# Hybrid decoder block with a PEER expert layer: row gathers serve 224 tokens instead of 192, and 288 instead of 320 go through all experts

## The chip, the cores and the metric

The kernel runs on one core of a Trainium2 chip. The metric is the device time of one launch in microseconds (us), lower is better. Five engines work side by side and meet through semaphores: TensorE (PE; its weight loads are listed as PEld), VectorE (DVE), ScalarE (ACT), GpSimd (POOL) and SyncE (SP, which issues nearly all plain DMAs). Each engine executes its own queue strictly in order. Sixteen DMA engines move data between HBM and the on-chip memory.

## What is computed

One decoder block for 512 tokens of width 2048, in float32. The first part (convolution and stick-breaking attention, gated and merged) isn't touched by the change. The second part is a PEER layer: every token picks 128 of 16384 experts (8 heads, 16 each), and adds what these experts give.

```python
def peer_ffn(x, wq, subkeys, u_table, v_table):
    q = jnp.einsum("btd,dq->btq", x, wq).reshape(b, t, 8, 2, 128)
    scores = jnp.einsum("bthsc,snc->bthsn", q, subkeys)
    top_s, top_i = lax.top_k(scores, 16)
    ...                                   # 16 best sums of both halves per head
    gate = jax.nn.softmax(sel_s, axis=-1)
    u = u_table[ib]                       # rows of the chosen experts, 128 per token
    hidden = jnp.einsum("td,thkd->thk", xb, u)
    act = jax.nn.gelu(hidden, approximate=False) * gb
    v = v_table[ib]
    return jnp.einsum("thk,thkd->td", act, v)

def reference(...):
    ...                                   # x: residual stream after the mixers
    xn = rmsnorm(x, norm_ffn)
    x = x + peer_ffn(xn, peer_wq, peer_subkeys, peer_u, peer_v)
    return rmsnorm(x, norm_final)
```

## The kernel before

Tokens are served by the PEER layer in two ways. The last 320 tokens (`ND`) go through **all** 16384 experts on TensorE, with a gate plane that is zero where a token didn't choose an expert. The first 192 tokens (`G0`) are served by **row gathers**: an indirect DMA brings, for 128 partitions at a time, one row of 2048 values of the table u or v per partition (1 MB, `fetch`, L685), and VectorE takes it in: for u a product with the token's vector, summed (L696), for v a multiply-add onto a running sum (L703).

The gathers come in two runs. The first serves tokens 0 to 127, one token per partition, 128 slots each: 128 gathers of u and then 128 of v. The second serves 64 tokens (`NG2`) with the slots of each token on two groups of partitions: 64 gathers of u, then 64 of v. At the end of a run `finish` adds the partition groups of the running sum (L757 copies one group's part by DMA, L758 adds it), takes the root mean square of the result with two ScalarE squares that write a PSUM tile of the ring `z` (L193), scales (L725) and stores. The ring `z` has two buffers that are handed out in program order, and the products with v need them too.

A gather needs one of four buffers `row` (`ROWS`); in the v part of a run the running sum holds one of them. The generator `gather` is advanced by `pump(rate)`: each step asks for one gather and takes in the one asked for a step earlier. A unit is 48 matmuls: either one expert tile of the up product (`up`, 16 blocks of the contraction times three products of high and low halves), or a pair of output blocks of the down product (`products`). The dense part has 128 up units and 128 down units: first the 64 up units of the chunks 0 to 7 (their result goes to memory without gates, L800), then the 64 down units of these chunks (`regain` fetches and gates the activations), and then eight chunks with 8 up and 8 down units each. Until the routing and the gate planes are done (unit 60), `pump` gets a rate of 1.0 gather per unit; after that the rate is chosen so that what is left is spread evenly over what is left of the dense part (`even`), less by a tenth up to unit 128. At the start of the last chunk's down product (`"last"`) what is left of the gathers is taken in.

Weights come as halves of 128 x 1024 (512 KB, L148) into seven buffers in the dense part (four `wraw`, three `spare`). ScalarE writes the rounded half `whi` (L133), VectorE the rest `wlo` (L134). Both have three buffers (`WHL`), so TensorE has at most three halves ahead, and each half feeds 24 matmuls. Nothing reaches TensorE in the dense part without a `wlo` from VectorE.

The order of each engine's queue isn't written by hand: a scheduler with a timeline of its own sets it when the program is built. The taking in of gathers is kept in program order among itself (`PIN`).

Of the kernel before, what the change touches and what calls it, by code (L numbers as in the profile page):

```python
# [8 lines left out]
F32 = mybir.dt.float32  # L9
# [21 lines left out]
NE = P // CHUNK  # L31
NG2 = 64
G0 = P + NG2
# [47 lines left out]
def block_kernel(ctx, tc, a, out, dbg=None):  # L81
# [77 lines left out]
    def behind(ins):  # L159
        """Queue ins on its engine behind the latest weight product."""  # L160
        tc.add_manual_dep(ins.ins, pe_last[0].ins.name, mybir.DependencyInfo(mybir.DependencyClass.NoSync, mybir.DependencyReason.DATA), reason="behind")
# [40 lines left out]
    def turn(x2, k, pin):  # L202
        """Two 128-column blocks of the pair of row tiles, transposed: [128, 2, 256]."""
        tp = accum()
        for kk in range(2):
            for tt in range(2):
                o = kk * NH + tt * P
                t = nc.tensor.transpose(tp[:, o:o + P], x2[tt][:, (k + kk) * P:(k + kk) * P + P], ident)
                if pin:
                    behind(t)  # L210
        return tp.rearrange("p (k t) -> p k t", k=2)

    def load_x(h):
        """Transposed tokens of one half times the norm's gains, split; 1 / rms of each token to inv."""
        t0 = h * NH
# [45 lines left out]
    def mixer(h, st, x):  # L261
        """Attention, convolution and their gated merge for one half of the tokens; the merge goes to
        md, and the last of it straight to the tiles of the output projection."""
        xhi, xlo, inv, first = x
# [156 lines left out]
    def suffix(pool, z, sp, seg, nj, W):  # L421
        """z minus the sums of sp over the keys from each key to the end."""
        last = nj - 1
# [21 lines left out]
    def outproj(pool, h, m, box):  # L445
        """Output projection and residual of 256 tokens."""
        t0 = h * NH
# [37 lines left out]
    def chain(pool, h, box, nhi, nlo, c0):  # L485
        """Normalized, transposed and split tokens of one half from column c0; tokens 0.. to xn2d."""
        x2 = box["x2"]
# [34 lines left out]
    def queries(pool, h, st, nhi, nlo, c0):  # L522
        """Product-key scores of 256 tokens, queued for the top 16 of each group."""
        for half in range(2):
            zt = [ztile() for _ in range(2)]
            for cg in range(8):
                ct = half * 8 + cg
                acc = accum()[:, :NH]
                yield from mmk(acc, wtile(a["wq"][ct]), lambda k: nhi[:, k, c0:c0 + NH], lambda k: nlo[:, k, c0:c0 + NH])
                pq = pool.tile([P, NH], F32, name="pq", bufs=2)  # L530
                mark(nc.scalar.copy(pq, acc))
                for tt in range(2):
                    nc.tensor.matmul(zt[tt][:, cg * P:cg * P + P], pq[:, tt * P:tt * P + P], sk[:, ct % 2], start=True, stop=True)
                yield
            both = None if h else row()
            for tt in range(2):
                sc = st["scp"].tile([P, 1024], F32, name="sc", bufs=4) if h else both[:, tt * 1024:tt * 1024 + 1024]
                nc.scalar.copy(sc, zt[tt])
                for cg in range(8):
                    st["topk"][2 * h + tt].append((sc[:, cg * P:cg * P + P], half * 8 + cg))  # L540
# [8 lines left out]
    def route(pool, tile_no, st):  # L549
        """Product-key routing of one 128-token tile: expert halves and gate of each slot."""  # L550
        ls = pool.tile([P, 2, 8, 2, 16], F32, name="ls", bufs=1)
# [10 lines left out]
        nc.vector.tensor_copy(tif, ti)  # L562
        # Of the 16 x 16 sums of two sorted lists only those with (a + 1) * (b + 1) <= 16 can be among
        # the first 16; rows a of widths 16, 8, 4, 1 hold them all, in the order of the full list.
        cand = spare()[:, 0:512].rearrange("p (h c) -> p h c", h=8)
# [14 lines left out]
        eg = pool.tile([P, 3, 8, 16], F32, name="eg", bufs=2)  # L580
        # Position in the compact list -> row a and column b.
        ic = pool.tile([P, 2, 8, 16], U32, name="ic", bufs=1)
# [51 lines left out]
    def gates(pool, eg, p0, b0, nb):  # L634
        """Dense gate planes of 16-token blocks b0.. from tokens on partitions p0.. of a routing tile."""
        for _ in range(GLAG):
# [39 lines left out]
    def gather_tile(pool, np_, nslot, idx, gate, load_x, load_acc, finish):  # L676
        """Row gathers for np_ partitions of (token, slot group), nslot slots each."""
        gx = late[1].tile([P, D], F32, name="gx", bufs=1)[0:np_]
# [49 lines left out]
    def gather(routes):  # L728
        idx = routes[0][0]
        yield from gather_tile(  # L730
            late[1], P, P, idx, st["gate"],
            lambda t: nc.sync.dma_start(t, xn2d[0:P]),
            lambda t: nc.sync.dma_start(t, x2d[0:P]),
            lambda t: finish_rows(t, slice(0, P), final_gain()))
        if not NG2:
            return
        S = P // (P // NG2)
        idx, eg = routes[1]
        idx2 = late[1].tile([P, S], I32, name="idx2")
        gate2 = late[1].tile([P, S], F32, name="gate2")  # L740
        for r in range(P // NG2):
            ps_, ss = slice(r * NG2, r * NG2 + NG2), slice(r * S, r * S + S)
            nc.sync.dma_start(idx2[ps_], idx[0:NG2, ss])
            nc.sync.dma_start(gate2[ps_], eg[0:NG2, 2, ss])

        def load_x(t):
            for r in range(P // NG2):
                nc.sync.dma_start(t[r * NG2:r * NG2 + NG2], xn2d[P:G0])

        def load_acc(t):  # L750
            nc.vector.memset(t, 0.0)
            nc.sync.dma_start(t[0:NG2], x2d[P:G0])

        def finish(t):
            for r in range(1, P // NG2):
                o = row()
                nc.sync.dma_start(o[0:NG2], t[r * NG2:r * NG2 + NG2])  # L757
                nc.vector.tensor_tensor(t[0:NG2], t[0:NG2], o[0:NG2], OP.add)  # L758
            finish_rows(t, slice(P, G0), final_gain())

        yield from gather_tile(late[1], P // NG2 * NG2, S, idx2, gate2, load_x, load_acc, finish)

    def dense(pool, st):
# [18 lines left out]
        def up(ch):  # L782
            """Expert activations of one chunk of expert tiles; without gates in the first chunks."""
            acts = []
# [22 lines left out]
        def regain(ch):  # L807
            """The activations of an early chunk with their gates, in steps that may be spread."""
            gt = gate_planes(ch)
# [93 lines left out]
    pumped = [0]  # L903
    rounds = 2 * P + (2 * (P // (P // NG2)) if NG2 else 0)

# [182 lines left out]
```

## Time and profile before

| | |
|---|---|
| time, three runs | 3630.88, 3636.36 and 3641.12 us, median 3636.36 |
| profiled execution, span from first to last instruction | 3629.1 us |
| TensorE, VectorE, ScalarE, GpSimd busy | 97%, 78%, 45%, 18% |
| DMA traffic | 1056.10 MB, of it 402.68 MB by gathers |

The profile lists no time of its own for the profiled execution beside the span; the span lies 1.8 us under the fastest of the three runs and 7.3 us under their median. Matmuls are pipelined, so a matmul's listed duration is longer than its share of time; what a matmul costs in a row of many is read from counts per stretch. The dense part begins at about 1724 us.

### The profile page before, as it was taken

The page shows a single profiled execution, that of the slowest core. Times are in us where ns is not written, and L with a number is a line of the kernel's source. Part 1 is how long each engine was busy: PE and PEld are TensorE (multiplying, and loading weights), DVE is VectorE, ACT ScalarE, POOL GpSimd, SP SyncE. Part 2 cuts the span into 40 slices and gives each one's busy share as a digit, 9 for nine tenths or more (in the row PEclk, how much of TensorE's full clock was granted, in tenths as well). Part 3 has the DMA queues.
Part 4 walks back from the last instruction along what each step waited for, and adds up shares of the span by engine and source line. Part 5 has one row for each costly group of instructions (what it writes and reads, how often), then busy time and mean ns, then how long its engine had stood idle before and what let it go on. Part 6 is the DMA issues. An engine that isn't in the chain of part 4 may idle for free.

```text
span 3629.1 us, 63343 instructions
## 1 busy us (share of the span) xinstructions
PE 3535.7 (97%) x25347; PEld 3420.6 (94%) x25347; DVE 2833.4 (78%) x4022; ACT 1621.6 (45%) x2277; POOL 644.8 (18%) x520
## 2 busy tenths in 40 slices
PE   9999999999999999889999999999999999999998
PEld 8999999798888999779999999999999999999997
DVE  6555557558988888788999886888887888888885
ACT  5444445445545543554337773333333333333334
POOL 0000000000234222012121111221122322322220
PEclk9999999999999999999999999999999999999998
DMA  5556666663788899899889889899988988889884
GB/s 194 170 176 219 214 216 216 198 193 127 267 306 332 335 344 356 313 331 344 295 324 334 309 317 364 326 358 337 341 328 327 358 328 336 325 338 349 326 319 150
DMA packets 297815, 1056.10 MB, mean 291 GB/s; under 512 B 36464, under 2 KB 109296, under 8 KB 243568
## 3 DMA queue, kind: packets, MB, share of 16 engines
q1 hardware_dynamic: 242224, 649.38, 51.3%
q0 software_dynamic: 55296, 402.68, 28.9%
q8 instruction: 199, 3.26, 0.3%
q14 instruction: 96, 0.79, 0.1%
HBM read 999.98 MB, written 51.38 MB: 290 GB/s over the span
## 4 chain that ended last, share of the span: by engine, by line
PE 73%; DVE 3%; DMA 2%; issue 2%; ACT 1%; POOL 0%; SPq 0%; DVEq 0%; ACTq 0%; POOLq 0%
PE pj L166 13%; PE pj L164 13%; PE pj L165 13%; PE z L164 9%; PE z L165 9%; PE z L166 9%; PE pj L668 2%; DVE wlo L134 1%; PE z L434 1%; PE tr L416 1%; DVE row L696 1%; DMA wraw<-in_w_mix 1%; DMA row<-in_u,idx 1%; PE z L397 0%; DMA gt<-gd 0%
## 5 line engine op out<-in xcount | busy, mean ns | idle before, releaser
L133 ACT ACTIVATE whi<-wraw 128x1024 fp32r<-128x1024 f32 x827 | 874.2, 1059 | 1229.3 <-PE pj L165 726.4
L134 DVE TENSOR_TENSOR wlo<-wraw,whi 128x1024 fp32r<-128x1024 f32 x827 | 1009.2, 1224 | 415.3 <-ACT whi L133 409.5
L166 PE MATMUL pj<-xhi,wlo 128*128 128x256 f32 x2560 | 719.7, 282 | 11.3 <-DVE wlo L134 11.1
L164 PE MATMUL pj<-xhi,whi 128*128 128x256 f32 x2560 | 721.6, 282 | 6.7 <-ACT whi L133 4.7
L165 PE MATMUL pj<-xlo,whi 128*128 128x256 f32 x2560 | 720.5, 282 | 0.0
L164 PE MATMUL pj<-dxhi,whi 128*128 128x320 f32 (+1 forms) x2304 | 710.0, 308 | 2.8 <-ACT whi L133 2.6
L166 PE MATMUL pj<-dxhi,wlo 128*128 128x320 f32 (+1 forms) x2304 | 704.1, 307 | 4.5 <-DVE wlo L134 4.5
L165 PE MATMUL pj<-dxlo,whi 128*128 128x320 f32 (+1 forms) x2304 | 705.8, 307 | 0.0
L164 PE MATMUL z<-ahi,whi 128*128 128x320 f32 x2048 | 631.0, 309 | 4.0 <-ACT z L193 2.9
L165 PE MATMUL z<-alo,whi 128*128 128x320 f32 x2048 | 631.5, 309 | 2.4 <-DVE alo L134 2.4
L166 PE MATMUL z<-ahi,wlo 128*128 128x320 f32 x2048 | 629.6, 309 | 1.8 <-DVE wlo L134 1.8
L166 PEld LDWEIGHTS pj<-xhi,wlo 128*128 128x128 f32 x2560 | 480.0, 188 | 21.5 <-DVE wlo L134 16.1
L164 PEld LDWEIGHTS pj<-xhi,whi 128*128 128x128 f32 x2560 | 481.7, 188 | 12.6 <-ACT whi L133 6.1
L165 PEld LDWEIGHTS pj<-xlo,whi 128*128 128x128 f32 x2560 | 481.4, 188 | 6.7 <-issue 5.3
L685 POOL DMA_INDIRECT row<-in_v,idx x192 | 286.7, 1493 | 1063.8 <-DVE row L703 448.9
L703 DVE SCALAR_TENSOR_TENSOR row<-row,gact 128x2048 f32<-128x2048 f32 x192 | 450.5, 2346 | 19.3 <-DMA row<-in_v,idx 19.3
L696 DVE SCALAR_TENSOR_TENSOR row<-row,gx 128x2048 f32<-128x2048 f32 x192 | 438.4, 2287 | 26.0 <-DMA row<-in_u,idx 25.0
L685 POOL DMA_INDIRECT row<-in_u,idx x192 | 290.8, 1515 | 857.8 <-DVE row L696 213.0
L166 PEld LDWEIGHTS pj<-dxhi,wlo 128*128 128x128 f32 x2304 | 433.3, 188 | 5.6 <-DVE wlo L134 5.6
L164 PEld LDWEIGHTS pj<-dxhi,whi 128*128 128x128 f32 x2304 | 434.5, 189 | 3.2 <-ACT whi L133 2.9
L165 PEld LDWEIGHTS pj<-dxlo,whi 128*128 128x128 f32 x2304 | 434.2, 188 | 0.0
L133 ACT ACTIVATE whi<-spare 128x1024 fp32r<-128x1024 f32 x197 | 208.8, 1060 | 414.8 <-PE z L165 263.8
(232 smaller groups left out, 5019.3 us busy)
## 6 DMA issues: line engine op xcount, KB each, us to landing
wraw<-in_w_in SPq DMA_DIRECT2D x320, 512.0 KB
wraw<-in_uT SPq DMA_DIRECT2D x187, 512.0 KB
wraw<-in_vT SPq DMA_DIRECT2D x128, 512.0 KB
spare<-in_vT SPq DMA_DIRECT2D x128, 512.0 KB
spare<-in_uT SPq DMA_DIRECT2D x69, 512.0 KB
wraw<-in_w_mix SPq DMA_DIRECT2D x64, 512.0 KB
wraw<-in_w_out SPq DMA_DIRECT2D x64, 512.0 KB
wraw<-in_wq SPq DMA_DIRECT2D x64, 512.0 KB
```

The costliest lines, as they stand in the source:

```text
L133: nc.scalar.activation(hi, src, AF.Copy)
L134: nc.vector.tensor_tensor(lo, src, hi.bitcast(F32), OP.subtract)
L164: nc.tensor.matmul(acc, shi, mhi, start=first, stop=False)
L165: nc.tensor.matmul(acc, shi, mlo, start=False, stop=False)
L166: pe_last[0] = nc.tensor.matmul(acc, slo, mhi, start=False, stop=last)
L416: nc.tensor.matmul(yps[hs, q0:], kv[j // 2][1][:, j % 2, hs], e[:, seg(j)], start=j == 0, stop=j == last, skip_group_check=True)
L434: nc.tensor.matmul(z[:, c], stat.bitcast(F32), src[:, c], start=False, stop=True, skip_group_check=True)
L668: behind(nc.tensor.matmul(gp[:, t * P:t * P + P], oh[:, t, 0], oh[:, t, 1], start=True, stop=True))
L685: ins = nc.gpsimd.indirect_dma_start(out=g, out_offset=None, in_=tab, in_offset=bass.IndirectOffsetOnAxis(ap=idx[0:np_, s:s + 1], axis=0))
L696: pin(nc.vector.scalar_tensor_tensor(g, g, 1.0, gx, OP.mult, OP.mult, accum_out=hid[:, s:s + 1]))
L703: pin(nc.vector.scalar_tensor_tensor(acc[0:np_], g, act[:, s:s + 1], acc[0:np_], OP.mult, OP.add))
```

## The change

A table `SEGS` takes the place of the two hand-written runs: three runs of (128 tokens, 1 partition group), (64 tokens, 2 groups) and (32 tokens, 4 groups). The third serves tokens 192 to 223 with 32 gathers of u and 32 of v, and its end has three copies and three additions of partition groups. There are 448 gathers instead of 384. `ND` falls from 320 to 288, so all matmuls of the up and the down product have 288 columns instead of 320, and the tiles of activations, gates and sums shrink alike. The gate planes have 18 blocks of 16 tokens instead of 20. The rate of `pump` after unit 60 follows from the count of gathers left: it was 1.00 rising to 1.04 per unit up to unit 128 and 1.17 after it, and is 1.31 rising to 1.37 and 1.53.

```diff
+SEGS = ((0, 0, 128), (1, 0, 64), (1, 64, 32))
-NG2 = 64
+NG2 = 96
 G0 = P + NG2
 ND = T - G0
...
     def gather(routes):
-        idx = routes[0][0]
-        yield from gather_tile(
-            late[1], P, P, idx, st["gate"],
...
-        yield from gather_tile(late[1], P // NG2 * NG2, S, idx2, gate2, load_x, load_acc, finish)
+        for tile_no, p0, n in SEGS:
+            R = P // n
+            rows = slice(tile_no * P + p0, tile_no * P + p0 + n)
+            idx, eg = routes[tile_no]
+            gate = st["gate"]
+            if R > 1:
...
+                for r in range(R):
+                    ps_, ss = slice(r * n, r * n + n), slice(r * n, r * n + n)
+                    nc.sync.dma_start(idx[ps_], src[p0:p0 + n, ss])
+                    nc.sync.dma_start(gate[ps_], eg[p0:p0 + n, 2, ss])
...
+            def finish(t):
+                for r in range(1, R):
+                    o = row()
+                    nc.sync.dma_start(o[0:n], t[r * n:r * n + n])
+                    nc.vector.tensor_tensor(t[0:n], t[0:n], o[0:n], OP.add)
+                finish_rows(t, rows, final_gain())
+
+            yield from gather_tile(late[1], P, n, idx, gate, load_x, load_acc, finish)
...
-    rounds = 2 * P + (2 * (P // (P // NG2)) if NG2 else 0)
+    rounds = sum(2 * n for _, _, n in SEGS)
```

The lines of the kernel after lie one or two below those of before (L703 is L705, L134 is L136). The scheduler sets another order too. The first place is VectorE's queue at the end of the first run of gathers, 128 tokens. `gact` marks a gathered row of v, `gx` one of u, `wlo` half a weight tile for TensorE. Before:

```order
L134 TENSOR_TENSOR alo<-hd,ahi 128x320
L703 SCALAR_TENSOR_TENSOR row<-row,gact 128x2048
L134 TENSOR_TENSOR wlo<-spare,whi 128x1024
L774 TENSOR_TENSOR hd<-hd,gt 128x320
L197 TENSOR_TENSOR ss<-ss 128x1
L134 TENSOR_TENSOR alo<-hd,ahi 128x320
L199 RECIPROCAL ss<-ss 128x1
L725 SCALAR_TENSOR_TENSOR row<-row,ss 128x2048
L134 TENSOR_TENSOR wlo<-wraw,whi 128x1024
```

After, at the same end (in the down product of chunk 7):

```order
L705 SCALAR_TENSOR_TENSOR row<-row,gact 128x2048
L136 TENSOR_TENSOR wlo<-spare,whi 128x1024
L705 SCALAR_TENSOR_TENSOR row<-row,gact 128x2048
L775 TENSOR_TENSOR hb<-hb,gt 128x288 x2
L136 TENSOR_TENSOR alo<-hb,ahi 128x288 x2
L705 SCALAR_TENSOR_TENSOR row<-row,gact 128x2048 x15
L199 TENSOR_TENSOR ss<-ss 128x1
L201 RECIPROCAL ss<-ss 128x1
L727 SCALAR_TENSOR_TENSOR row<-row,ss 128x2048
L698 SCALAR_TENSOR_TENSOR row,hid<-row,gx 128x2048 x2
L136 TENSOR_TENSOR wlo<-wraw,whi 128x1024
```

Where single gathers stood between weight halves, 16 rows of v, the end of the run and two rows of u now stand between one `wlo` and the next. The second place is VectorE's queue at the end of the 64-token run, which before is also the last of the gathers, ahead of the last chunk's down product. Before:

```order
L134 TENSOR_TENSOR wlo<-spare,whi 128x1024
L774 TENSOR_TENSOR hd<-hd,gt 128x320
L134 TENSOR_TENSOR alo<-hd,ahi 128x320
L758 TENSOR_TENSOR row<-row 64x2048
L134 TENSOR_TENSOR wlo<-wraw,whi 128x1024
L197 TENSOR_TENSOR ss<-ss 128x1
L774 TENSOR_TENSOR hd<-hd,gt 128x320
L134 TENSOR_TENSOR wlo<-spare,whi 128x1024
L199 RECIPROCAL ss<-ss 128x1
L134 TENSOR_TENSOR alo<-hd,ahi 128x320
L725 SCALAR_TENSOR_TENSOR row<-row,ss 128x2048
L134 TENSOR_TENSOR wlo<-wraw,whi 128x1024
```

After, at the end of the 64-token run (in the down product of chunk 12):

```order
L136 TENSOR_TENSOR wlo<-wraw,whi 128x1024
L705 SCALAR_TENSOR_TENSOR row<-row,gact 128x2048
L136 TENSOR_TENSOR wlo<-spare,whi 128x1024
L705 SCALAR_TENSOR_TENSOR row<-row,gact 128x2048 x28
L759 TENSOR_TENSOR row<-row 64x2048
L199 TENSOR_TENSOR ss<-ss 128x1
L201 RECIPROCAL ss<-ss 128x1
L727 SCALAR_TENSOR_TENSOR row<-row,ss 128x2048
L136 TENSOR_TENSOR wlo<-wraw,whi 128x1024
```

Here 28 rows of v stand in a row, and the whole end of the run behind them, ahead of the next `wlo`. The third place is the end of the 32-token run, in the same queue ahead of the last chunk's down product, where before the rows just shown stood. After:

```order
L136 TENSOR_TENSOR alo<-hd,ahi 128x288
L136 TENSOR_TENSOR wlo<-spare,whi 128x1024
L705 SCALAR_TENSOR_TENSOR row<-row,gact 128x2048 x13
L759 TENSOR_TENSOR row<-row 32x2048 x3
L199 TENSOR_TENSOR ss<-ss 128x1
L201 RECIPROCAL ss<-ss 128x1
L727 SCALAR_TENSOR_TENSOR row<-row,ss 128x2048
L136 TENSOR_TENSOR wlo<-wraw,whi 128x1024
L839 TENSOR_TENSOR dacc<-z,dacc 128x576
```

Here 13 rows of v, three additions and the end of the run stand between two weight halves. Before, no more than two gathers stand between two neighbouring `wlo` in the dense part. After, beside these places, there are four in one place (unit 30) and three in another (unit 141). Outside these three places VectorE's queue of after holds 1.05 gathers per unit from unit 64 to 121 and 1.17 from 122 to 250; before it holds 1.00 and 1.16.

## Rows read from the trace of the kernel before

**Rows 1.** The page: busy time, share and instructions of TensorE, VectorE.

```profile
PE 3535.7 (97%) x25347; PEld 3420.6 (94%) x25347; DVE 2833.4 (78%) x4022; ACT 1621.6 (45%) x2277; POOL 644.8 (18%) x520
```

**Rows 2.** The page: the chain that ended last, shares by engine.

```profile
PE 73%; DVE 3%; DMA 2%; issue 2%; ACT 1%; POOL 0%; SPq 0%; DVEq 0%; ACTq 0%; POOLq 0%
```

**Rows 3.** Windows: length, busy us (instructions) per engine, granted clock, DMA share, GB/s.

```profile
1724.00:1899.00 175.00, 172.18 (x1162) 171.62 (x1161) 173.41 (x468) 66.20 (x81) 31.24 (x23) 0.99 0.86 312
1899.00:2183.00 284.00, 283.44 (x2054) 283.19 (x2054) 245.13 (x490) 199.15 (x421) 47.49 (x34) 1.00 0.87 317
2183.00:2245.00 62.00, 57.66 (x379) 56.88 (x378) 39.11 (x38) 21.26 (x32) 12.83 (x8) 0.97 1.01 379
2245.00:2705.00 460.00, 454.71 (x3081) 451.58 (x3080) 393.98 (x370) 159.76 (x185) 92.82 (x66) 1.00 0.92 339
2705.00:3497.00 792.00, 789.13 (x5377) 788.44 (x5377) 646.99 (x590) 282.26 (x345) 211.91 (x129) 1.00 0.89 335
```

**Rows 4.** Windows: matmuls of 256 columns, then of 320 columns.

```profile
400.00:500.00 100.00, 100.00 (x851) 100.00 (x850) 57.63 (x70) 42.54 (x52) 0.00 (x0) 1.00 0.72 224
3200.00:3300.00 100.00, 100.00 (x684) 100.00 (x683) 83.91 (x66) 35.03 (x42) 25.56 (x17) 1.00 0.89 334
```

**Rows 5.** Waits from 2705 to 3497 us: total, times, longest.

```profile
ACT whi L133 <- PE z L165: 268.1, 105, 5.0
```

**Rows 6.** Groups of matmuls from 1899 to 2183 us: gate planes.

```profile
L668 PE MATMUL pj<-spare 128*128 128x128 f32 x512 | 69.0, 275 | 0.6 <-DVE spare L651 0.6
```

**Rows 7.** DMA queues from 2245 to 2705 us: packets, MB, share of 16 engines.

```profile
q1 hardware_dynamic: 44763, 86.81, 53.3%
q0 software_dynamic: 9443, 68.72, 37.9%
```

**Rows 8.** DMA queues from 2705 to 3497 us, same columns.

```profile
q1 hardware_dynamic: 50643, 129.22, 45.2%
q0 software_dynamic: 18581, 135.31, 43.1%
```

**Rows 9.** Windows of the fullest DMA, columns as in rows 3.

```profile
3180.00:3190.00 10.00, 10.00 (x70) 10.00 (x69) 7.93 (x8) 3.92 (x7) 2.78 (x2) 1.00 1.01 419
3210.00:3220.00 10.00, 10.00 (x70) 10.00 (x70) 7.21 (x8) 3.43 (x4) 2.59 (x2) 1.00 1.00 345
1200.00:1400.00 200.00, 196.94 (x1625) 192.40 (x1624) 162.81 (x173) 89.22 (x109) 43.77 (x34) 1.00 0.94 346
```

**Rows 10.** Groups on VectorE from 2705 to 3497 us: busy us, mean ns.

```profile
L703 DVE SCALAR_TENSOR_TENSOR row<-row,gact 128x2048 f32<-128x2048 f32 x65 | 152.5, 2346 | 0.0
...
L134 DVE TENSOR_TENSOR wlo<-wraw,whi 128x1024 fp32r<-128x1024 f32 x112 | 136.9, 1222 | 67.1 <-ACT whi L133 65.7
```

**Rows 11.** Timeline, end of the first run, ScalarE then VectorE: start, us.

```profile
2755.20 1.03 ACT L193 ACTIVATE z<-row 128x1024 f32<-128x1024 f32 x1 [0.40 <-DVE row L703]
...
2757.77 1.28 ACT L198 ACT_TABLE_LOAD   x1
...
2759.60 2.35 DVE L725 SCALAR_TENSOR_TENSOR row<-row,ss 128x2048 f32<-128x2048 f32 x1
```

**Rows 12.** Timeline, end of the second run: the copy and the addition.

```profile
3536.68 0.48 SPq L757 DMA_DIRECT2D row<-row  x1
...
3542.09 2.28 DVE L758 TENSOR_TENSOR row<-row 64x2048 f32<-64x2048 f32 x1
```

**Rows 13.** Windows around the end of the first run.

```profile
2750.00:2755.00 5.00, 3.53 (x25) 3.27 (x23) 5.00 (x5) 2.82 (x4) 1.58 (x1) 1.00 0.70 252
2755.00:2760.00 5.00, 3.60 (x24) 3.60 (x25) 2.93 (x7) 4.13 (x7) 1.19 (x1) 1.00 1.00 372
```

**Rows 14.** Windows around a longer stop of TensorE.

```profile
1485.00:1490.00 5.00, 0.00 (x0) 0.00 (x0) 1.68 (x2) 0.70 (x2) 0.94 (x1) 0.54 1.02 406
1490.00:1495.00 5.00, 4.08 (x17) 3.79 (x18) 4.16 (x4) 2.52 (x3) 0.00 (x0) 0.50 1.01 398
1495.00:1500.00 5.00, 5.00 (x30) 4.46 (x29) 4.82 (x11) 3.00 (x6) 0.00 (x0) 0.94 0.60 229
```

More of the change, by code (lines that the diff above doesn't have):

```diff
@@ L728, in gather @@
     def gather(routes):
-        idx = routes[0][0]
-        yield from gather_tile(
-            late[1], P, P, idx, st["gate"],
[L732 to L759, printed above, removed]
@@ L761, in gather, with load_x, load_acc @@
-        yield from gather_tile(late[1], P // NG2 * NG2, S, idx2, gate2, load_x, load_acc, finish)
+        for tile_no, p0, n in SEGS:
[4 more added lines that the diff above has]
+            if R > 1:
+                src, idx = idx, late[1].tile([P, n], I32, name=f"idx{n}")
+                gate = late[1].tile([P, n], F32, name=f"gate{n}")
+                for r in range(R):
+                    ps_, ss = slice(r * n, r * n + n), slice(r * n, r * n + n)
+                    nc.sync.dma_start(idx[ps_], src[p0:p0 + n, ss])
+                    nc.sync.dma_start(gate[ps_], eg[p0:p0 + n, 2, ss])
+            def load_x(t):
+                for r in range(R):
+                    nc.sync.dma_start(t[r * n:r * n + n], xn2d[rows])
+            def load_acc(t):
+                if R > 1:
+                    nc.vector.memset(t, 0.0)
+                nc.sync.dma_start(t[0:n], x2d[rows])
+            def finish(t):
[5 more added lines that the diff above has]
+            yield from gather_tile(late[1], P, n, idx, gate, load_x, load_acc, finish)
```

## The prediction

> **What bounds the kernel now.** I read the page first. TensorE is busy 97% of the span, VectorE 78% [rows 1], and 73% of the chain that ended last is TensorE's [rows 2]. The reader is to see that no other engine holds more than 3% of that chain. A busy TensorE need not be at its peak, so I went on to the windows by stage [rows 3]. Five stages make up the dense part. In 1724 to 1899 us VectorE is the full one, 173.4 of 175 us: routing. In 1899 to 2183 us TensorE is busy 283.4 of 284 us: gate planes beside the up product. The 62 us after it have the DMA engines at 1.01, and TensorE misses 4 us. In 2245 to 2705 us (64 down units, 7.19 us each) TensorE misses 5 us at a DMA share of 0.92. In 2705 to 3497 us (112 units, 7.07 us each) it misses 3 of 792 us, at 0.89. So TensorE bounds most of it, with the DMA engines close behind: the windows also show 394 us of VectorE in 460 and 647 in 792, 86% and 82%.
>
> What a matmul costs follows from counts: 100 us hold 851 with 256 columns or 684 with 320, so 117.5 and 146.2 ns [rows 4]; 5377 in 792 us give 147.3 ns [rows 3]. With 288 columns I take the middle of 117.5 and 147.3, 132.4 ns. 48 of them make a unit of 6.36 us, 0.71 less than now.
>
> **What the change gives.** Six terms, by stage.
> 1. Before unit 0: the order is the same up to the first gate planes, of which 32 tokens fall away, two listed matmuls each. 512 such matmuls share a stretch with 1536 wide ones [rows 6]; taking 147.3 ns for the wide ones, the 284 us leave 0.11 us for each. 64 of them: 7 us if TensorE is the last there, which it isn't throughout. I take 5 (0 to 9).
> 2. Units 0 to 53: the first 24 are VectorE's and win nothing. In the next 284 us 1536 matmuls get shorter by 14.9 ns, 23 us; VectorE (245 of 284) and DMA (0.87) then become nearly full [rows 3], so 16 (10 to 22).
> 3. Units 54 to 63, where the DMA engines are full already: 2 (0 to 5).
> 4. Units 64 to 120, 57 units. Here I ask what the DMA engines need. Gathers take 37.9% of 460 us over 64 units, 2.72 us of full engines per unit; all else 53.3%, 3.83 us [rows 7]. After, VectorE's queue holds 1.05 gathers per unit outside the long rows instead of 1.00, 2.86 us, and the smaller activations and planes leave about 3.74 of the rest. Together 6.60 us, more than TensorE's 6.36. How full can they be while TensorE runs? Over 200 us at a share of 0.94 TensorE was 98.5% busy [rows 9]. I take 0.96: 6.87 us per unit, 0.32 below 7.19, 18 us. Bounds: 34 at 1.00, 1 at 0.92.
> 5. Units 122 to 249, 128 units. Gathers 43.1% of 792 us over 112 units, 3.05 us; the rest 45.2%, 3.20 us [rows 8]. After 3.08 and 3.18, together 6.26; at 0.96 this is 6.52 us against 7.07: 70 us. Bounds: 91 where TensorE's 6.36 decides, 35 at 0.92 (6.80). VectorE's 5.78 us per unit (647 over 112) stay below all of these.
> 6. Units 250 to 255, no gathers left: 6 x 0.71, 4 us.
>
> Sum of the gains: 115 us (50 to 165).
>
> **What the change costs.** The gathers that were asked for at the higher rate aren't taken in at that rate: the three long rows in VectorE's queue hold 16, 28 and 13 rows of v. TensorE needs a `wlo` behind each of them. Its cover is what is split already: three halves of 24 matmuls, 3.18 us each, so 9.5 us at most. ScalarE is usually waiting for TensorE to free a `whi` (268 us in 105 waits [rows 5]), so these buffers tend to be full; I take 8 us (5 to 9.5).
>
> The price of one gather in such a row: VectorE alone needs 2.35 us [rows 10]. The DMA must bring 1.049 MB: gathers moved 135.31 MB in 43.1% of 792 us, 396 GB/s at a full share [rows 8], or 2.65 us; the full 10 us windows run from 345 to 419 GB/s [rows 9], 3.04 to 2.50 us. Three buffers and an issue between each consumption and the next landing make it no faster, so 2.8 us, near the 2.65, with 2.35 and 3.04 as ends. The first three rows of a stretch have landed and cost 2.35.
>
> The end of a run stands behind its row: from ScalarE's first square to VectorE's scaling 4.4 us, the scaling 2.35 [rows 11], then one `wlo`, 1.2 [rows 10]. An addition of groups takes 2.3 us; the copy ahead of it was issued 5.4 us before the addition began [rows 12], which is an upper bound, and I take 3, copies side by side.
> - First row: 3 x 2.35 + 13 x 2.8 = 43.5; four small steps 2; end 6.8; two rows of u 4.7; `wlo` 1.2: 58, less cover 50.
> - Second: 3 x 2.35 + 25 x 2.8 = 77; copy and addition 5.3; end and `wlo` 8: 90, less cover 82.
> - Third: 3 x 2.35 + 10 x 2.8 = 35; copy and three additions 9.9; end and `wlo` 8: 53, less cover 45.
>
> TensorE idles 177 us. After a stop its granted clock is at the lower level: 0.50 for 5 us and 0.94 for five more after the stop at 1485 us [rows 14], some 3 us lost, so 9 for three. Before, the first run's end cost 2.9 us (10 us less 3.53 and 3.60) [rows 13], which this replaces. Net 183 us. With 2.35 per gather, full cover and less clock it is 153; with 3.04, 5 us of cover and 5 us of clock each it is 210.
>
> Instructions to issue cost nothing by themselves: the 64 further gathers are POOL's, busy 18% [rows 1], hidden behind the DMA they start.
>
> **Sum.** 183 less 115 is +68 us. These are differences within one profiled execution with a span of 3629.1 us, 7.3 us under the median of the runs; I add them to the median 3636.4: **3704 us**.
>
> A rule is weighed here. The rows show 10 us windows at 419 GB/s, and gathers at 396 for a full share [rows 8, 9]. The Trainium skill, page "DMA: Bandwidth & Descriptors", section "Where 436 GB/s comes from", says that for transfers between HBM and the on-chip memory the HBM side binds at about 358 GB/s per core. By that rule, an estimate, a gather in a row would cost 2.93 us, and the sum would rise by 6 us for the rows. The trace disagrees: these rows stand above 358. So I keep 2.8.
>
> **Rivals.**
> - *TensorE's saving wins, faster.* Place: the 128 units after the first row. If the DMA engines can be kept at 1.00 there, TensorE decides and the gains are 165 us; with the rows at VectorE's pace, 153, the time is 3624. For: gathers rarely keep VectorE waiting now, and full 10 us windows exist [rows 9]. Against: no window of 100 us or more with TensorE at full pace has a share above 0.94 to 0.95. It decides only if the gains exceed what the rows cost; at gains of 165 the rows must be below 2.45 us per gather, below the 2.65 that the gathers' own DMA time gives. With my gains no price above 2.35 does it.
> - *The DMA engines bound everything, slower still.* If they only reach the 0.92 of 2245 to 2705 us [rows 3], terms 4 and 5 shrink to 1 and 35, gains to 62, and the time is 3757. For: 67 MB more in less time. Against: 0.94 was sustained over 200 us.
> - *Rows and gains cancel, within 0.3%.* Gains near 145 and rows near 150, for instance with 0.98 full and 2.35 us per gather: 3641.
>
> **How the numbers follow.** Forecast 0.58, DMA rival 0.21, cancelling 0.11, faster 0.10. A measurement of this kernel can tell 0.3%, 11 us, from no change. So faster 0.10, same 0.11, slower 0.79. Taking all lows gives 3624, all highs 3796; 8 times in 10 I expect **3632 to 3780**.
>
> **What the profile after would show.** Three stops of TensorE of some 45 to 80 us, each under a stretch of VectorE with nothing but `row<-row,gact`, one near unit 121, one near 205, one ahead of the last chunk; the granted clock low behind each. Between them units of 6.4 to 6.9 us and a DMA share of 0.93 to 0.97. I am wrong on the rows if TensorE's longest stop is under 30 us or a gather in a row takes under 2.4 or over 3.2 us, and wrong on the gains if units stay at 7.0 us or more between the rows, or come to 6.36.

## The result and the profile after

The changed kernel takes 3760.7 us (3756.9 to 3764.2), the kernel before 3635.1: a ratio of 1.034 (95% interval 1.033 to 1.036), slower by 126 us, where +68 had been forecast; the time lies in the upper part of the range that I gave (3632 to 3780). The profiled execution has a span of 3762.5 us, 133.4 more than before. The page after, busy time by engine, the chain by engine, and three groups (line, engine, operation, count | busy us, mean ns | idle us ahead and its releaser):

```profile
PE 3385.5 (90%) x25283; PEld 3261.9 (87%) x25283; DVE 2961.5 (79%) x4078; ACT 1608.9 (43%) x2245; POOL 725.8 (19%) x584
...
PE 15%; DMA 3%; issue 2%; DVE 2%; POOL 1%; ACT 0%; POOLq 0%; DVEq 0%; ACTq 0%
...
L166 PE MATMUL z<-ahi,whi 128*128 128x288 f32 x2048 | 614.4, 301 | 240.8 <-ACT z L195 223.3
...
L705 DVE SCALAR_TENSOR_TENSOR row<-row,gact 128x2048 f32<-128x2048 f32 x224 | 525.7, 2347 | 88.7 <-DMA row<-in_v,idx 87.9
```

TensorE was 97% busy [rows 1] and is 90% busy. The third line says where it went: 223.3 us of idle time ahead of one product with v, ended by a ScalarE square that writes the ring `z`. Against [rows 10], VectorE's wait for gathered rows of v, which was 0.0 in the 792 us shown there, is now 87.9 us. The waits in three windows, 2595 to 2670, 3220 to 3340 and 3610 to 3692 us (engine, line, what it waited for: total us, times, longest):

```profile
PE z L166 <- ACT z L195: 55.4, 1, 55.4
...
PE z L166 <- ACT z L195: 106.7, 1, 106.7
ACT z L195 <- DVE row L759: 104.5, 1, 104.5
DVE row L705 <- DMA row<-in_v,idx: 27.4, 24, 2.8
DVE row L759 <- DMA row<-row: 4.3, 1, 4.3
...
PE z L166 <- ACT z L195: 61.2, 1, 61.2
```

Three stops, at 2605, 3226 and 3621 us. Windows inside the second, and the stretches ahead of it (columns as in [rows 3]):

```profile
2225.00:2604.00 379.00, 361.17 (x2633) 357.42 (x2633) 339.73 (x331) 137.24 (x163) 83.30 (x58) 0.97 0.96 360
...
2723.00:3226.00 503.00, 483.83 (x3580) 480.39 (x3578) 427.92 (x406) 185.12 (x230) 131.57 (x87) 0.98 0.94 354
...
3240.00:3250.00 10.00, 0.00 (x0) 0.00 (x0) 7.05 (x3) 0.00 (x0) 2.82 (x3) 0.50 0.98 355
3250.00:3260.00 10.00, 0.00 (x0) 0.00 (x0) 7.06 (x3) 0.00 (x0) 6.84 (x4) 0.50 0.76 288
```

In the stop VectorE takes in three gathers in 10 us and is idle for three of them, the granted clock lies at 0.50 (1.2 GHz), and the DMA share swings. The end of this stop in the timeline (start, us, engine, line [idle ahead, releaser]):

```profile
3322.49 2.35 DVE L705 SCALAR_TENSOR_TENSOR row<-row,gact 128x2048 f32<-128x2048 f32 x1 [1.43 <-DMA row<-in_v,idx]
...
3329.18 2.28 DVE L759 TENSOR_TENSOR row<-row 64x2048 f32<-64x2048 f32 x1 [4.33 <-DMA row<-row]
3331.50 1.03 ACT L195 ACTIVATE z<-row 128x1024 f32<-128x1024 f32 x1 [104.55 <-DVE row L759]
...
3332.70 0.61 PE L166 MATMUL z<-ahi,whi 128*128 128x288 f32 x1 [106.71 <-ACT z L195]
...
3335.52 2.35 DVE L727 SCALAR_TENSOR_TENSOR row<-row,ss 128x2048 f32<-128x2048 f32 x1
```

TensorE goes on right behind the first square, 2.8 us ahead of the scaling and well ahead of the next `wlo`. So what it waits for is not the weight behind the row, as I had said, but the PSUM ring: buffers are handed out in program order, the squares at the run's end are the next to get one, and the products behind them queue up although their weights are split already.

### The profile page after: what moved, and what is told of

Same layout as the page of the kernel before. It is cut to its first block, busy times and chain, and to the rows that moved or that the text cites. A ratio compares the mean times of both kernels' runs of the same rounds, so it can differ in the third digit from the quotient of the medians.

```text
span 3762.5 us, 63416 instructions
## 1 busy us (share of the span) xinstructions
PE 3385.5 (90%) x25283; PEld 3261.9 (87%) x25283; DVE 2961.5 (79%) x4078; ACT 1608.9 (43%) x2245; POOL 725.8 (19%) x584
## 3 DMA queue, kind: packets, MB, share of 16 engines
q0 software_dynamic: 64512, 469.79, 32.8%
## 5 line engine op out<-in xcount | busy, mean ns | idle before, releaser
L136 DVE TENSOR_TENSOR wlo<-wraw,whi 128x1024 fp32r<-128x1024 f32 x827 | 1008.1, 1223 | 342.9 <-ACT whi L135 337.6
L166 PE MATMUL z<-ahi,whi 128*128 128x288 f32 x2048 | 614.4, 301 | 240.8 <-ACT z L195 223.3
L168 PE MATMUL pj<-dxhi,wlo 128*128 128x288 f32 (+1 forms) x2304 | 682.6, 298 | 13.2 <-DVE wlo L136 13.2
L166 PE MATMUL pj<-dxhi,whi 128*128 128x288 f32 (+1 forms) x2304 | 686.3, 298 | 8.1 <-ACT whi L135 7.8
L167 PE MATMUL pj<-dxlo,whi 128*128 128x288 f32 (+1 forms) x2304 | 674.2, 293 | 0.0
L168 PE MATMUL z<-ahi,wlo 128*128 128x288 f32 x2048 | 607.2, 299 | 18.7 <-DVE wlo L136 18.6
L167 PE MATMUL z<-alo,whi 128*128 128x288 f32 x2048 | 612.2, 300 | 0.0
L166 PEld LDWEIGHTS z<-ahi,whi 128*128 128x128 f32 x2048 | 392.7, 192 | 244.4 <-ACT z L195 224.0
L705 DVE SCALAR_TENSOR_TENSOR row<-row,gact 128x2048 f32<-128x2048 f32 x224 | 525.7, 2347 | 88.7 <-DMA row<-in_v,idx 87.9
L687 POOL DMA_INDIRECT row<-in_v,idx x224 | 332.3, 1483 | 1069.0 <-DVE row L705 532.2
L698 DVE SCALAR_TENSOR_TENSOR row<-row,gx 128x2048 f32<-128x2048 f32 x224 | 511.0, 2286 | 33.3 <-DMA row<-in_u,idx 33.2
```

Source lines behind the costliest of these rows:

```text
L136: nc.vector.tensor_tensor(lo, src, hi.bitcast(F32), OP.subtract)
L166: nc.tensor.matmul(acc, shi, mhi, start=first, stop=False)
L167: nc.tensor.matmul(acc, shi, mlo, start=False, stop=False)
L168: pe_last[0] = nc.tensor.matmul(acc, slo, mhi, start=False, stop=last)
L687: ins = nc.gpsimd.indirect_dma_start(out=g, out_offset=None, in_=tab, in_offset=bass.IndirectOffsetOnAxis(ap=idx[0:np_, s:s + 1], axis=0))
L698: pin(nc.vector.scalar_tensor_tensor(g, g, 1.0, gx, OP.mult, OP.mult, accum_out=hid[:, s:s + 1]))
```

## The experiments

Two theories stood at first. **Lag**: gathers are asked for faster than they are taken in, and TensorE stops where the order makes it wait for that backlog. **DMA**: the 67 MB more are what costs, wherever TensorE waits. A third, the ring `z` alone, came from the rows just shown.

**Squares in another ring.** The changed kernel with the run's end writing PSUM ring `tr` in place of `z`:

```diff
-        for c in range(2):
-            junk = ztile()
-            nc.scalar.activation(junk, x[:, c * 1024:c * 1024 + 1024], ...)
+        for c in range(4):
+            junk = trtile()
+            nc.scalar.activation(junk, x[:, c * 512:c * 512 + 512], ...)
+        nc.vector.tensor_tensor(ss[:, 0:2], ss[:, 0:2], ss[:, 2:4], OP.add)
...
```

> The squares at the end of a run write the PSUM ring tr instead of the ring z, so the down products no longer queue behind the end of a run for a z buffer. In VectorE's queue the three long rows of v are then gone from the middle, and 61 gathers (29 of u, 32 of v) stand behind the last wlo. Lag theory (the order takes gathers in more slowly than they are asked for, and whoever waits for the end of a run waits for what is left over; each leftover gather costs about 3.3 us in v and 2.8 us in u): the three stops of TensorE (55, 107 and 61 us) vanish, and a tail of some 29 x 2.8 + 32 x 3.3 + 15 = 200 us without TensorE appears: 3720 to 3740 us. Ring theory (the ring z alone makes the stops, the gathers would otherwise fit beside TensorE's work): about 3761 - 235 = 3530 us, and no tail.

Measured: 3774.8 us, 1.038 of before (1.036 to 1.040), 35 us above what the lag theory expected and far from the ring theory. The first three lines are waits from 3515 us on, the windows after them the stretch up to the last weight and the stop behind it:

```profile
PE tr L845 <- ACT tr L195: 195.2, 1, 195.2
ACT tr L195 <- DVE row L760: 116.0, 1, 116.0
...
ACT gact L702 <- DVE row L699: 84.6, 1, 84.6
```

```profile
2225.00:3518.00 1293.00, 1243.21 (x9171) 1232.69 (x9170) 1099.67 (x1032) 483.90 (x589) 282.32 (x207) 0.98 0.93 346
3525.00:3719.00 194.00, 0.00 (x0) 0.00 (x0) 147.66 (x94) 2.65 (x8) 104.57 (x57) 0.51 0.87 327
```

The three stops vanish, and one of 195 us behind the last weight takes their place, with 29 gathers of u and 32 of v left over. It is 28 us shorter than the three together, and yet the kernel takes 14 us longer. So the ring sets where TensorE stops, and hardly how long in all. The ring theory falls; the lag theory holds in kind, though its size was 35 us short.

**No third run**, 288 columns kept, so that 32 tokens get no experts:

```diff
-SEGS = ((0, 0, 128), (1, 0, 64), (1, 64, 32))
+SEGS = ((0, 0, 128), (1, 0, 64))
```

> 288 columns without the third run: tokens 192 to 223 get nothing from the experts and their output rows aren't written. The row that is left in VectorE's queue is one of 8 gathers ahead of the last chunk's down product. Lag theory: the narrower matmuls give units of about 6.7 us (64 to 127) and 6.5 us (128 to 247) at a DMA share of 0.93 to 0.97, 120 us less than before, and the row of 8 costs some 30 to 40: 3540 to 3560 us. DMA theory (the DMA engines stay near the shares of 0.89 to 0.92 that they had, so narrower matmuls can't be used): 3615 to 3636 us.

Measured: 3559.3 us, 0.979 (0.977 to 0.981). Stops of 14.9 and 37.0 us are left, at the ends of its two runs. The fewer columns alone are worth 74 us. That is less than the 100 or so that the faster units show, because of these stops.

**The third run on top of 320 columns**, its result thrown away:

```diff
 SEGS = ((0, 0, 128), (1, 0, 64), (1, 64, 32))
-NG2 = 96
+NG2 = 64
...
-        nc.sync.dma_start(out[rows], x[0:n])
+        nc.sync.dma_start(thrown if rows.start == G0 else out[rows], x[0:n])
```

> The third run alone: 320 columns as before, and the 32 tokens 192 to 223 are served by gathers as well, their result thrown into a scratch tensor. VectorE's queue has rows of 16, 22 and 9 gathers of v. Lag theory: units between the rows at before's 7.1 us, rows at 3.3 us per gather with the ends of the runs, three stops of 55, 85 and 45 us: 3636 + 190 = 3815 to 3840 us. DMA theory (67 MB more, and the engines had a tenth of 1300 us free): 3670 to 3700 us.

Measured: 3842.9 us, 1.058 (1.056 to 1.059), 3 us above what lag expected and 143 above DMA; its stops are 56.1, 86.9 and 42.6 us. The third run alone costs 210 us, which is 3.3 us for each of its 64 gathers. 210 less 74 is 136, near the 126 of both together.

**No long rows**: each splitting of a weight in the dense part is queued behind the taking in of the gather two back, so that nothing piles up (`taken` lists the instructions that take a gather in; the dependency sets an order and no wait of its own):

```diff
+    KEEP = 2
...
-        split(raw, hi, lo)
+        nc.scalar.activation(hi, raw, AF.Copy)
+        ins = nc.vector.tensor_tensor(lo, raw, hi.bitcast(F32), OP.subtract)
+        if spare_ok[0] and len(taken) > KEEP:
+            tc.add_manual_dep(ins.ins, taken[-1 - KEEP].ins.name, ...)
...
```

> The whole change, but a wlo of the dense part may not be queued ahead of a gather's consumption that was asked for more than two gathers earlier. The long rows are gone: VectorE's queue holds 10 to 13 gathers per 8 units throughout, never more than two between neighbouring wlo behind unit 30. If the rows were the whole loss: 3761 - 235 = 3526 us. If the gathers' DMA time counts wherever they stand: 1.34 and 1.53 gathers per unit need 7.4 and 7.2 us of full DMA engines, 7.7 and 7.5 us per unit at 0.96: about 3690 us, still slower than before, with the DMA share at 0.95 or more from unit 64 to 250 and no stop of TensorE over 10 us.

Measured: 3733.2 us, 1.027 (1.025 to 1.029). This was the hardest miss, 43 us above the later of the two expectations: no long row is left, no stop is longer than 17.3 us, and only 28 us came back of the 223. The dense part over 184 units, from the end of the first down unit to the end of the first of the last chunk's down product, before, after and here:

```profile
2245.00:3554.00 1309.00, 1300.80 (x8843) 1296.72 (x8842) 1089.43 (x1005) 467.84 (x567) 311.61 (x200) 1.00 0.90 336
```

```profile
2225.00:3692.00 1467.00, 1200.49 (x8833) 1191.44 (x8834) 1234.05 (x1111) 471.09 (x575) 386.19 (x264) 0.91 0.92 347
```

```profile
2232.00:3669.00 1437.00, 1259.31 (x8829) 1231.12 (x8829) 1220.96 (x1106) 472.32 (x574) 444.03 (x262) 0.94 0.93 352
```

TensorE has 100 us less to do than before, and the part is 128 us longer without one long row. So the rows are the form that the loss takes, not all of its cause. New theory: this part has to move 510 MB instead of 439 (2225 to 3692 against 2245 to 3554 us), and even without stops it runs against the transfers. The waits of this run don't show that directly: in its dense part VectorE waited 16.8 us for gathered rows of v and ScalarE some 25 us for weights and activations from DMA, while TensorE waited 98.8 us for `wlo` and VectorE was busy 1221 of 1437 us. Eight further runs are on that theory, and on the order by itself.

**A fifth buffer** for every fifth gather, in the space that the narrower tiles left:

```diff
+            nth[0] += 1
-            g = row()[0:np_]
+            g = (st['gtp'].tile([P, D], F32, name='fifth', bufs=1)
+                 if spare_ok[0] and nth[0] % 5 == 0 else row())[0:np_]
```

> After, with one more buffer that every fifth gather of the part through all experts goes to. The order that comes out has rows of 14 and 6 consumptions, one of 4 and six of 3 instead of 18, 28 and 13, so two things change at once: buffers and rows. Round-trip theory (a gather in a long row costs 3.34 us because three buffers share a round trip of 7.2 us and a consumption of 2.36): with a fourth buffer in part of the turns a gather in the row of 14 takes 2.5 to 2.8 us. If the stops are all that is lost, about 223 us of them become 14 x 2.7 + 11 = 49 and 6 x 2.7 + 11 = 27, and the time is 3761 - 150 = 3600 to 3640. DMA theory, new: of the 1467 us from 2225 to 3692 the queues were busy 0.92, 1350 us; with no share above 0.97 seen over a long stretch this part cannot end in less than 1350 / 0.97 = 1392 us, so the time stays at 3685 or above, 3690 to 3740, and the units between the rows become slower than the 6.85 and 6.63 us of after as the stops shrink; a gather in the row stays at 3.2 to 3.4 us.

Measured: 3711.9 us, 1.021 (1.019 to 1.023), the best of the versions that do all the work with 224 gathered tokens, and still slower than before. Its dense part, and waits in its row of 14:

```profile
2227.00:3638.00 1411.00, 1215.47 (x8830) 1197.44 (x8831) 1222.82 (x1109) 466.72 (x574) 478.46 (x263) 0.94 0.93 361
```

```profile
PE z L167 <- ACT z L196: 62.8, 1, 62.8
...
POOL row L689 <- DVE row L707: 34.0, 6, 7.8
DVE row L707 <- DMA row<-in_v,idx: 12.9, 5, 4.6
```

The floor held: the part took 1411 us, above the 1392 expected at the least. With the stops taken out, its units 64 to 127 took 7.26 us and 128 to 247 took 6.92, slower than the 6.88 and 6.67 of the changed kernel, as that theory expected. A gather in the row still took 3.30 us (14 taken in from 3239.03 to 3285.16 us), but GpSimd still waited 34 us for buffers of the old ring, because only each fifth gather has the new one. So this run doesn't tell whether buffers or transfers set that price.

**No long rows and the fifth buffer**, both edits together:

> The run without overtaking (no long rows, 3733 us) with the fifth buffer added. If its remaining loss came from three buffers (VectorE waiting for a gather's round trip at the head of its queue), 3640 to 3690 us. If the transfers themselves bound the part (the floor of 1392 us from 2225 on), 3690 to 3735 us at a DMA share of 0.94 to 0.97.

Measured: 3730.5 us, 1.028 (1.025 to 1.031). The buffer is worth nothing there. Its first 495 us of the dense part:

```profile
2225.00:2720.00 495.00, 449.99 (x3206) 441.95 (x3205) 444.11 (x421) 170.00 (x201) 191.05 (x89) 0.96 0.97 371
```

The fullest 300 us of this run, and the fullest 1000 us of any run, which are those of the fifth buffer with long rows:

```profile
2169.00:2469.00 300.00, 270.77 (x1932) 266.15 (x1932) 268.41 (x249) 102.59 (x128) 113.23 (x54) 0.96 1.00 385
```

```profile
2178.00:3178.00 1000.00, 914.94 (x6643) 899.85 (x6643) 878.41 (x823) 345.27 (x425) 334.64 (x185) 0.97 0.96 371
```

At 371 GB/s 510 MB take 1374 us, 65 more than the whole dense part before. At 385, with the engines full throughout, they would take 1324, still 15 more. Both are estimates.

**Half the bytes, first try**: each gather fetches 64 whole rows, and VectorE takes them in on 64 partitions.

```diff
-indirect_dma_start(out=g, ..., in_offset=...(ap=idx[0:np_, s:s + 1], axis=0))
+indirect_dma_start(out=g[0:h], ..., in_offset=...(ap=idx[0:h, s:s + 1], axis=0))
```

> After, with each gather fetching 64 rows instead of 128 (0.5 MB instead of 1 MB), consumed on 64 partitions in the same VectorE time per instruction; the experts of the other half are left out. The order that comes out has no long row either (one of 6, two of 3). Both theories expect TensorE's own pace here, 188 units x 6.5 us instead of 1467 us from the first lag on: 3761 - 245 = 3500 to 3540 us. Its distance to the run without rows that fetches everything (3733 us) is what the bytes alone cost: 190 to 230 us if the transfers are the bound, under 60 us if VectorE's order is.

> The kernel before, with each gather fetching 64 rows instead of 128, consumed on 64 partitions; the experts of the other half are left out. Of the 1312 us from 2185 to 3497 TensorE was busy 1299, so if matmuls alone bound the kernel before, nothing moves: 3615 to 3633 us. If its DMA share of 0.90 already cost something, 3560 to 3610 us.

Measured: 3908.5 us, 1.074 (1.072 to 1.077), and on the kernel before 3856.6 us, 1.062 (1.060 to 1.064). Both missed by far, the wrong way: half the bytes made both kernels slower than everything else here. From 2340 to 3820 us, in the changed kernel:

```profile
2340.00:3820.00 1480.00, 1260.32 (x8983) 1236.43 (x8982) 1227.59 (x1119) 474.23 (x582) 508.87 (x270) 0.94 0.98 252
```

A DMA share of 0.98 with 252 GB/s: the engines were fuller with fewer bytes. The next run has the same bytes over 128 partitions.

**Half the bytes, second try**: half rows into all 128 partitions (the table read as twice as many rows of half the length), the half taken in twice so that VectorE has its full length.

```diff
-indirect_dma_start(out=g, out_offset=None, in_=tab, ...)
+indirect_dma_start(out=g[:, D // 2:D], out_offset=None, in_=tab.rearrange("r (b c) -> (r b) c", b=2), ...)
-scalar_tensor_tensor(g, g, 1.0, gx, ...)
+scalar_tensor_tensor(two(g), twice(g), 1.0, two(gx), ...)
```

> After, with each gather fetching half a row (1024 elements) into all 128 partitions: 0.5 MB instead of 1 MB, over as many partitions as before, which the gathers of 64 whole rows were not. VectorE consumes the half row twice, so its instruction is as long as before; half of each expert is left out. The order has no long row (one of 6, two of 3). DMA theory: without the long rows and with 510 - 160 = 350 MB in the stretch that had 510, TensorE sets the pace, 188 units x 6.5 us: 3500 to 3560 us, so the bytes cost some 170 to 230 us against the run without rows that fetches everything (3733 us). Theory of VectorE's order (the rows are gone, its queue is as full as before): 3670 to 3733 us. If what counts is the number of row descriptors and not their bytes: also 3690 or more, at a DMA share of 0.9.

> The kernel before, with each gather fetching half a row into all 128 partitions; half of each expert is left out. From 2185 on TensorE was busy 1299 of 1312 us, so there is at most 13 us to gain there; the part ahead of it has the gathers and the weights too. If matmuls alone bound the kernel before: 3615 to 3633 us. If its DMA share of 0.90 costs something ahead of that part: 3580 to 3615 us. It shows how near the kernel before stood to the limit that the changed one ran into.

Measured: 3627.6 us, 0.9985 (0.9975 to 0.9995) for the changed kernel, and 3678.6 us, 1.013 (1.012 to 1.015) for the kernel before. The dense part of the first, and the queue of its gathers on the page, beside that of the 64-row run (packets, MB, share of 16 engines over the span):

```profile
2256.00:3554.00 1298.00, 1194.53 (x8825) 1185.38 (x8824) 1209.77 (x1104) 466.95 (x574) 487.55 (x262) 0.96 0.81 283
```

```profile
q0 software_dynamic: 64512, 234.91, 18.5%
```

```profile
q0 software_dynamic: 35840, 234.91, 26.1%
```

The dense part falls from 1437 to 1298 us, 11 less than before's 1309, with as much work for VectorE as ever (1210 against 1221) and an order without long rows in both. So half the gathered bytes are worth up to 139 us there. Not all of that need be the bytes: only the 1437 are with the strict order, which the last run below prices at 35 us on this part of the kernel before, and that would leave some 100; and a half row may also land and free its buffer sooner. Half rows under the strict order were not run, so the size is open. The sum stayed above the expected 3500 to 3560 us for two reasons: the dense part began 39 us late (1760 against 1721 us), and stops of 31.6 and 21.2 us were left. In the first 64 units of that part another limit shows:

```profile
2256.00:2710.00 454.00, 419.77 (x3072) 415.63 (x3071) 425.19 (x402) 161.09 (x190) 167.56 (x85) 0.97 0.82 288
```

At a DMA share of 0.82 they took 454 us, and VectorE was busy 94% of them. Over the whole part VectorE has 1210 us of work and TensorE 1195, in the changed kernel 1234 and 1200, before 1089 and 1301. So the change also makes VectorE the fuller of the two, and a version that was free of the transfers would meet VectorE's queue next.

The late start also makes the second run slower than before (unit 0 at 1763 instead of 1724). From 1000 us up to there VectorE waits 82.0 us for rows of u, against 24.4 before; why fewer bytes let it wait longer there I did not find out. On the whole that run is inconclusive, but its dense part, 184 units again, gives an answer:

```profile
2279.00:3594.00 1315.00, 1303.53 (x8832) 1296.75 (x8831) 1082.30 (x996) 468.66 (x564) 398.73 (x200) 1.00 0.72 252
```

It took 1315 us at a DMA share of 0.72, where the kernel before took 1309 at 0.90. Half the gathered bytes were worth nothing there: TensorE was busy 1304 and 1301 us. The transfers didn't bind this part before the change.

**Half the dose** (16 tokens in the third run, 304 columns) with the strict order, and **the strict order alone**, on the kernel before (the edit of the run without long rows). The edit of the dose:

```diff
-SEGS = ((0, 0, 128), (1, 0, 64), (1, 64, 32))
-NG2 = 96
+SEGS = ((0, 0, 128), (1, 0, 64), (1, 64, 16))
+NG2 = 80
```

> Half the dose: a third run of 16 tokens (208 gathered, 304 columns through all experts), with the order that lets no splitting overtake a consumption two back, so no long rows. If only long rows cost, half of the columns' gain of 100 us is left: 3575 to 3605 us, which would beat both kernels. DMA theory: the stretch from the first lag on moves (444 + 510) / 2 = 477 MB, busy 477 / 0.376 = 1268 us, at a share of 0.94 1349 us against 1312 before; less 15 us ahead of it: 3640 to 3675 us. Either way it stands between before and the run without overtaking at full dose (3733 us).

> The kernel before (192 gathered, 320 columns) with the order in which no splitting overtakes a consumption two back. The kernel before has no long rows that this could remove, so the run prices the order by itself. If the order is free (theory by which the 3733 and 3735 us of the two changed kernels with it are the price of transfers near their limit alone): 3625 to 3650 us. If the strict order costs by itself, because a splitting then waits in VectorE's queue behind a consumption whose gather is late: 3670 to 3730 us, and then what those two runs lost beyond their transfers is the order's.

Measured: 3735.2 us, 1.029 (1.027 to 1.031), and 3661.7 us, 1.008 (1.006 to 1.010). The dense part of the first, then of the second:

```profile
2250.00:3660.00 1410.00, 1285.19 (x8832) 1272.97 (x8832) 1172.46 (x1063) 475.36 (x575) 388.17 (x231) 0.95 0.90 337
```

```profile
2245.00:3589.00 1344.00, 1317.27 (x8859) 1311.98 (x8858) 1093.92 (x1005) 473.67 (x568) 350.60 (x200) 0.99 0.89 328
```

Both theories on the first missed by 60 us or more, and no clear limit shows: its DMA share is only 0.90. The second says why the order can't be held innocent: it costs 31 us by itself, between the two expectations. In its dense part TensorE waited 18.1 us for `wlo`, where it had waited 1.8. That a splitting then stands behind a gather that is late fits, but VectorE waited only 7.4 us for gathered rows there, so it is not shown to be the way. About 30 us of the first stay unexplained; its longest stop, 27.1 us, stands ahead of the last chunk's down product. No run with more than 192 gathered tokens and all of the work done beat the kernel before.

## Why the prediction was half right

**Direction and outline held.** Three stops at the three long rows, the clock low in them, and faster units between: all there, and the longest is the middle one. What ended the stops was another wait than I had said, the ring `z` in place of the next `wlo`.

**The stops were mis-sized**: 55.4, 106.7 and 61.2 us, 223 in all, where 50, 82 and 45 were forecast. For the middle one, term by term:
- 28 gathers took 93.6 us (3231.22 to 3324.85), 3.34 each, instead of 77 at 2.8. The bound of 3.04 didn't hold either, and by my own sign (over 3.2 us) I was wrong on the rows. The price was taken from DMA windows in which many transfers overlap; in the row each gather waits for its buffer, is issued, and lands 5.4 to 7.7 us later, mostly some 7. These pieces stand in the chain through the stop (start, us, what):

```profile
3240.19 7.29 DMA row<-in_v,idx
...
3304.80 7.72 DMA row<-in_v,idx
3312.61 2.36 DVE row L705
3314.97 0.26 issue
3315.23 7.17 DMA row<-in_v,idx
3322.49 2.36 DVE row L705
```

Three buffers that each go through 7.2 of transfer, 2.4 of taking in and 0.3 give (7.2 + 2.4 + 0.3) / 3 = 3.3 us, which fits. So does the DMA share of 0.81 over this row (VectorE's line L705 alone: length, busy us, granted clock, DMA share, GB/s):

```profile
3231.00:3325.00 94.00, 65.92 (x28) 0.50 0.81 298
```

It is argued from this chain, not shown: the run that was to show it didn't settle it. The first row took 3.02 per gather, at a share of 0.96 (2615 to 2660 us), so there the transfers themselves may have set the pace; the third took 3.47, at 0.73 (3624 to 3680 us, copies included).
- Copy and addition took 4.33 + 2.28 = 6.6 instead of 5.3.
- The step that failed outright is the cover. I gave TensorE 8 us of split weights; it stopped 5.2 us *before* the row began, since the next buffer of the ring `z` was the squares' already. In return it needed only 1.2 us behind the addition instead of 8. 93.6 + 6.6 + 1.2 + 5.2 = 106.6.

**The gains** were close. With the stops taken out, units 64 to 127 came at 6.88 us (6.87 forecast) and units 128 to 247 at 6.67 (6.52), at shares of 0.96 and 0.94 (0.93 to 0.97 forecast); units 0 to 63 gave 16.6 us (18 forecast) and unit 0 began 3.9 us earlier (5). What is left of the gains after the clock's loss is 223 - 3 - 133 = 87 us of the profiled span (3 for the end of the first run before), where 115 - 9 = 106 was forecast. So rows and gains missed the same way, the rows by 46 us and the gains by 19: nothing cancelled. One reading of mine was off: from 3155 to 3255 us of the kernel before, the DMA share is 0.96 with TensorE busy throughout, where I had said that none exceeds 0.94 to 0.95.

**The place where the argument was too short** is the reading of the limit. The DMA rival gave 3757 us, close to the measured time, with a chance of 0.21, and not by the way it went: between the rows the share did rise to 0.94 to 0.96. But I had treated rows and DMA as two ways to lose. The runs speak for taking them as one: the gathers that the dense part can't bring in time are the lag, and a change of order mostly moves where it is paid (in three places, in one of 195 us, or spread over the units). Bytes over the whole part point there at once: 510 MB at 371 GB/s are 1374 us, above the 1309 us of before, whatever the order. They don't give the size: the part took 1411 to 1467 us in the changed kernel and its versions with the strict order, the fifth buffer or both, and VectorE's work and the strict order have a share in that which no run isolates.

The rule that I had set aside comes nearer over long stretches. Over the windows of 379 to 1467 us shown above, the runs that gather whole rows with 224 tokens moved 346 to 371 GB/s. The Trainium skill, page "DMA: Bandwidth & Descriptors", section "Where 436 GB/s comes from", puts the limit of the HBM side at about 358 GB/s per core; by the page, an estimate, the 510 MB take 1424 us. These windows lie within 4% of it, but it is not a bound here: 300 us ran at 385 GB/s and the 10 us windows of [rows 9] at up to 419, and the fifth buffer's part was through in 1411 us.

**What stays open**: how the 3.34 us of a gather in a row divide between the round trip and transfers that share the engines, some 30 us of the run at half dose, how much of the 139 us is bytes and how much order, and the late start with half rows.

## What to carry to other kernels

Before moving work from a compute engine to transfers, divide the bytes of the whole stretch by the highest rate that was seen over a stretch of like length, not by that of the best 10 us; if that exceeds the stretch as it is, a better order is unlikely to save it. Add up the work of each engine in the stretch as well: here VectorE's came out above TensorE's. Where a queue is set by a scheduler, look in it for rows of one kind of work, and for what TensorE shares with that work besides weights: here a PSUM ring decided where it stopped. When a long stop is taken out and the time hardly moves, the stop was where the loss was paid, not its cause.

## What the runs showed of the hardware that I had not expected

- A gather of 64 whole rows is not half a gather of 128. The same 234.91 MB took 26.1% of 16 engines over a span of 3916 us as 64 rows of 2048 values, and 18.5% over 3624 us as 128 rows of 1024. Per gather (448 of them) that is 2.28 and 1.50 us of all engines, against 2.75 for the full 1 MB (32.8% of 3762.5 us). The other transfers got slower beside it too: from 2225 to 3640 us the queue of the plain DMAs moved 226.83 MB in 56.2% of 16 engines, against 226.26 MB in 43.6% in the changed kernel.
- A single gather under load takes 5.4 to 7.7 us of transfer in the chain through the stop, two to three times the 2.35 us in which VectorE takes it in. With few buffers this belongs in the price beside the rate; how the two divide here is open.
- The copy of one partition group (64 x 2048 values) between two buffers made VectorE wait 4.33 us.
